# Two-layer hybrid trunk on one core: folding the two modulation vectors into one tile by partition halves before the transposes

## The chip, the cores and the metric

The kernel runs on one core of one Trainium2 chip. The metric is the device time of one execution in microseconds (us); lower is better. The kernel before takes 2441.62 us, the median of 3 runs.

## The reference

One inference step of a trunk of two layers. A layer modulates its normalised input, projects it into three parallel mixers (differential attention, mLSTM, neighbourhood attention), gates and sums their outputs, adds the result to the residual stream, and then runs a squared-ReLU MLP in the same way. There are 640 token rows: 512 of a denoising sample and 128 of a prompt, each group with its own modulation vector (conditioning `c` and `c_ctx`). Cut to what bears on the change:

```python
def layer(x, mod, lp, lam_init, ctx):
    sh1, sc1, g1, sh2, sc2, g2 = jnp.split(mod, 6, axis=-1)
    h = rmsnorm(x, lp['norm1']) * (1 + sc1) + sh1
    ...                                  # three mixers, gates -> merged
    x = x + g1 * (merged @ lp['w_out'])
    h2 = rmsnorm(x, lp['norm2']) * (1 + sc2) + sh2
    u = jnp.square(jax.nn.relu(h2 @ lp['w_ff1'] + lp['b_ff1']))
    x = x + g2 * (u @ lp['w_ff2'] + lp['b_ff2'])
```

`mod` is the product of a conditioning vector of 1024 with `w_mod` (1024 x 6144 for each layer) plus `b_mod`, once for each of the two vectors. The MLP is 1024 to 4096 to 1024.

## The kernel before

One program for one core, written with a framework that takes the order of a Python walk as a wish and lets a scheduler place the instructions on the engines. Every matrix product is split: weights and activations are kept as a rounded high part and a low rest, and each product is three matmuls (lines 191 to 193 in `gemm_a`, with the weights stationary, and 210 to 212 in `gemm_b`, with the activations stationary). A block of weights arrives as a 1 MB tile `raw`, of which there are two buffers for all loads of weights; ACT casts it to `whi` (L217) and DVE subtracts to get `wlo` (L218). Loads are issued by SP, in the order that the scheduler set.

**The modulation** is a matrix product with two columns, and it is done mostly on DVE, in the background. `mod_first` does the first 2048 columns of layer 0 at the start. The 20 chunks of 512 columns that are left (8 of layer 0, 12 of layer 1) go through `mod_chunk_dve`. For each chunk two `raw` tiles of `w_mod` are loaded (L325); each holds four slices of 128 rows by 512 columns. Into two accumulators `macc`, one for each vector, DVE adds slice times the vector's value in that row: 2 multiplications (L331) and 14 multiply-adds (L333) a chunk. What is left is the sum over the 128 partitions. PE transposes each accumulator in four blocks of 128x128 (L340, eight transposes a chunk) into a PSUM tile of the tag `t`, DVE reduces each tile along its free axis (L341, two a chunk), and `mod_store` adds the bias and writes into `modc` (L314).

The chunks are one generator, `bg`, made in `run`. Each `background()` runs it to its next `yield`. It is called from two kinds of place: in the mixers before the units whose number is in `BG_UNITS`, and in the feed-forward stage from `ff1` at the places in `FF1_BG` and from `ff2` after the row tiles in `FF2_BG`. The chunks of layer 0 run in layer 0's mixers, those of layer 1 in layer 0's feed-forward; layer 1's own stages have no background work. A chunk of layer 0 has two steps and a chunk of layer 1 four, as the `yield`s in it stand.

**The feed-forward** of a layer goes chapter by chapter. A chapter `ch` has two items `ff1(ch, 0)` and `ff1(ch, 2)`, of 4 gemms each, and a pair of items `ff2(ch, 0)` and `ff2(ch, 1)` of 5 gemms each (one for each of the five row tiles t). A gemm of ff2 is 12 matmuls of 512 columns; its result is scaled by DVE into a `tmp` tile of two buffers (L1577) and added to the residual rows by POOL (L1578). A gemm of ff1 is 24 matmuls of 256 or 384 columns; ACT applies ReLU and a square (L1490, L1491) and DVE makes the low part (L1492, L1493).

**PSUM** matters here. In this stage the gemms take their result tile alternately from the tag `t` (two buffers) and from the tag `mm` (two buffers), see `mm_ps`. The transposes of a chunk take theirs from `t` too (`t_ps`). Buffers of a tag go round in the order in which tiles are asked for, so a matmul that opens a tile waits until the engine that reads the tile two places earlier in that tag has read it. In the mixers the tag `mm` serves the projections; its tiles are read, among others, by the gates' tanh on ACT (L470, in `unit_gate`).

Of the kernel before, what the change touches and what calls it, by code (L numbers as in the profile page):

```python
# [14 lines left out]
ALU = mybir.AluOpType  # L15
AX = mybir.AxisListType
# [3 lines left out]
P = 128  # L20
# [66 lines left out]
class Builder:  # L87
# [229 lines left out]

    def mod_chunk_dve(self, l, n):

        nc, I = self.nc, self.I  # L320
        acc = [self.T(self.wp, [P, 512], F32, "macc", 2) for _ in range(2)]
        for kh in range(2):
            raw = self.T(self.wp, [P, 2048], F32, "raw", NRAW)
            r3 = raw.rearrange("p (k c) -> p k c", k=4)
            nc.sync.dma_start(r3, I["w_mod"][l, n, kh])  # L325
            for k in range(4):
                kk = kh * 4 + k
                for v in range(2):
                    s = self.cc3[:, v, kk:kk + 1]
                    if kk == 0:  # L330
                        nc.vector.tensor_scalar_mul(acc[v], r3[:, k, :], s)  # L331
                    else:
                        nc.vector.scalar_tensor_tensor(acc[v], r3[:, k, :], s, acc[v], op0=ALU.mult, op1=ALU.add)  # L333
                if kk in ((1, 3, 5) if l else (3,)):
                    yield
        red = self.st(8)
        for v in range(2):
            tp = self.t_ps()
            for j in range(4):
                nc.tensor.transpose(tp[:, j * P:(j + 1) * P], acc[v][:, j * P:(j + 1) * P], self.ident)  # L340
            nc.vector.tensor_reduce(red[:, 4 * v:4 * v + 4], tp.rearrange("p (j c) -> p j c", j=4), axis=AX.X, op=ALU.add)  # L341
        self.mod_store(l, n, red.rearrange("p (v j) -> p v j", v=2))
        yield

# [185 lines left out]
    def drive(self, units, stages, rate, w, tail, free=False):  # L530
# [41 lines left out]
        while cur[1] is not None:  # L572
# [13 lines left out]
            self.units_run += 1  # L586
            if self.units_run in BG_UNITS:
                self.background()
# [1150 lines left out]
ML_FIRST = 2  # L1739
CARRY = 3  # L1740
LAG1, LAG2 = 1, 1
FF1_BG, FF2_BG = ((0, 0), (1, 256)), (1, 3)
BG_UNITS = range(8, 42, 2)
WARM = (0, 0, 0, 0, 6, 2, 1, 1)
NSL, NOT, NV = 16, 12, 9

# [84 lines left out]
```

## Time and profile before

| | |
|---|---|
| median of 3 runs | 2441.62 us (2440.91 to 2443.32) |
| the profiled execution | 2439.98 us |
| its span in the profile | 2438.2 us |
| mean granted TensorE clock | 0.999 |
| chain that ended last, by engine | PE 91%, DVE 3%, DMA 2%, ACT 1%, issue 1%, POOL 1% |
| bytes moved by DMA | 286.51 MB, mean 118 GB/s |

All durations below come from the one profiled execution. The span is what lies between the first and the last recorded instruction; the execution's own time is 1.8 us longer, and the median of the runs is 1.6 us above that. Matmuls are pipelined: the duration of one overlaps the next, so what one costs is the distance between starts. Layer 0's feed-forward chapters lie at about 860 to 1165 us, the chapters of layer 1 that are read below at 2042 to 2320 us.

### The profile page before, as it was taken

To read this page: it belongs to the slowest core of one execution; us is meant where nothing else is said; L and a number is where in the kernel's file an instruction comes from. 1 tells how busy PE (TensorE), PEld (TensorE's weight loads), DVE (VectorE), ACT (ScalarE), POOL (GpSimd) and SP (SyncE) were. 2 spreads that over 40 slices of the span, in tenths; PEclk is the share of its full clock that TensorE was granted. 3 is DMA by queue.
4 is the path that set the end of the run, shared out by engine and by line. 5 is a ranking of instruction groups with operands and counts; after the bars stand their busy time and mean duration, and the time that the engine had idled before them with its cause. 6 is when DMAs were issued, how large, how long until landed. Compare 5 with 4: busy or idle time off the path is not lost.

```text
span 2438.2 us, 39566 instructions
## 1 busy us (share of the span) xinstructions
PE 2405.4 (99%) x15872; PEld 2260.3 (93%) x15872; DVE 1534.2 (63%) x2880; ACT 959.6 (39%) x2056; POOL 448.2 (18%) x521
## 2 busy tenths in 40 slices
PE   7999999999999999999999999999999999999998
PEld 4999999999998989999989999999999989999997
DVE  6667888667555899899475547664453564444444
ACT  4333454444434322222354325454553253222242
POOL 0011001233200333332010010102240012333301
PEclk9999999999999999999999999999999999999999
DMA  7333323433372344444233231223232722212221
GB/s 272 112 103 127 126 99 116 133 122 136 120 259 97 121 139 143 151 142 154 86 125 118 94 100 66 83 78 122 67 128 85 277 73 84 87 69 72 84 70 60
DMA packets 73703, 286.51 MB, mean 118 GB/s; under 512 B 9888, under 2 KB 21248, under 8 KB 49968
## 3 DMA queue, kind: packets, MB, share of 16 engines
q1 hardware_dynamic: 73520, 283.99, 33.6%
q8 instruction: 124, 2.03, 0.3%
q14 instruction: 59, 0.48, 0.1%
HBM read 257.60 MB, written 26.35 MB: 116 GB/s over the span
## 4 chain that ended last, share of the span: by engine, by line
PE 91%; DVE 3%; DMA 2%; ACT 1%; issue 1%; POOL 1%; SPq 0%; POOLq 0%; DVEq 0%; ACTq 0%
PE mm L191 15%; PE mm L192 14%; PE mm L193 14%; PE mm L212 5%; PE mm L211 5%; PE mm L210 5%; PE t L210 3%; PE t L212 3%; PE t L211 3%; PE t L193 3%; PE t L192 3%; PE t L191 3%; PE t L1067 2%; PE t L1356 1%; PE s L1337 1%
## 5 line engine op out<-in xcount | busy, mean ns | idle before, releaser
L191 PE MATMUL mm<-act,whi 128*128 128x384 f32 (+1 forms) x2128 | 682.4, 321 | 2.4 <-DVE act L643 2.4
L192 PE MATMUL mm<-act,whi 128*128 128x384 f32 (+1 forms) x2128 | 670.9, 315 | 0.0
L193 PE MATMUL mm<-act,wlo 128*128 128x384 f32 (+1 forms) x2128 | 670.8, 315 | 0.0
L217 ACT CAST whi<-raw 128x1024 fp32r<-128x1024 f32 x296 | 310.9, 1050 | 896.5 <-PE mm L192 420.0
L218 DVE TENSOR_TENSOR wlo<-raw,whi 128x1024 fp32r<-128x1024 f32 x296 | 377.1, 1274 | 360.5 <-ACT whi L217 306.0
L191 PEld LDWEIGHTS mm<-act,whi 128*128 128x128 f32 x2128 | 402.4, 189 | 6.7 <-DVE act L643 3.1
L192 PEld LDWEIGHTS mm<-act,whi 128*128 128x128 f32 x2128 | 402.8, 189 | 0.0
L193 PEld LDWEIGHTS mm<-act,wlo 128*128 128x128 f32 x2128 | 402.0, 189 | 0.0
L1578 POOL TENSOR_TENSOR x<-x,tmp 128x512 f32<-128x512 f32 x120 | 194.0, 1623 | 452.0 <-DVE tmp L1577 446.6
L210 PE MATMUL mm<-whi,act 128*128 128x512 f32 (+2 forms) x768 | 260.8, 340 | 0.0
L212 PE MATMUL mm<-whi,act 128*128 128x512 f32 (+2 forms) x768 | 257.3, 335 | 0.0
L211 PE MATMUL mm<-wlo,act 128*128 128x512 f32 (+2 forms) x768 | 257.2, 335 | 0.0
L333 DVE SCALAR_TENSOR_TENSOR macc<-raw,cc,macc 128x512 f32<-128x512 f32 x280 | 228.7, 859 | 21.6 <-DMA raw<-w_mod 21.4
L210 PE MATMUL t<-whi,act 128*128 128x512 f32 (+2 forms) x448 | 167.1, 373 | 0.1
L212 PE MATMUL t<-whi,act 128*128 128x512 f32 (+2 forms) x448 | 166.7, 372 | 0.0
L211 PE MATMUL t<-wlo,act 128*128 128x512 f32 (+2 forms) x448 | 166.4, 371 | 0.0
L193 PE MATMUL t<-act,wlo 128*128 128x256 f32 (+1 forms) x560 | 160.0, 286 | 0.0
L192 PE MATMUL t<-act,whi 128*128 128x256 f32 (+1 forms) x560 | 159.9, 286 | 0.0
L191 PE MATMUL t<-act,whi 128*128 128x256 f32 (+1 forms) x560 | 159.8, 285 | 0.0
L212 PEld LDWEIGHTS mm<-whi,act 128*128 128x128 f32 x768 | 145.5, 189 | 14.2
L210 PEld LDWEIGHTS mm<-whi,act 128*128 128x128 f32 x768 | 145.5, 189 | 14.1
L211 PEld LDWEIGHTS mm<-wlo,act 128*128 128x128 f32 x768 | 145.5, 189 | 14.0
(301 smaller groups left out, 4107.5 us busy)
## 6 DMA issues: line engine op xcount, KB each, us to landing
raw<-w_in SPq DMA_DIRECT2D x64, 1024.0 KB
raw<-w_ff SPq DMA_DIRECT2D x64, 1024.0 KB
raw<-w_mod SPq DMA_DIRECT2D x48, 1024.0 KB
mgd<-act SPq DMA_DIRECT2D x32, 320.0 KB
act<-mgd SPq DMA_DIRECT2D x32, 320.0 KB
raw<-w_out SPq DMA_DIRECT2D x8, 1024.0 KB
gr<-gd SPq DMA_DIRECT2D x12, 512.0 KB
act<-rd SPq DMA_DIRECT2D x16, 320.0 KB
```

What stands on the lines that cost most here:

```text
L191: nc.tensor.matmul(o, wh, ah, start=(k == 0), stop=False)
L192: nc.tensor.matmul(o, wh, al, start=False, stop=False)
L193: nc.tensor.matmul(o, wl, ah, start=False, stop=(k == nk - 1))
L210: nc.tensor.matmul(o, ah, wh, start=(first and k == 0), stop=False)
L211: nc.tensor.matmul(o, ah, wlo, start=False, stop=False)
L212: nc.tensor.matmul(o, al, wh, start=False, stop=(last and k == nk - 1))
L217: self.nc.scalar.copy(hi, src)
L218: self.nc.vector.tensor_tensor(lo, src, hi.bitcast(F32), op=ALU.subtract)
L333: nc.vector.scalar_tensor_tensor(acc[v], r3[:, k, :], s, acc[v], op0=ALU.mult, op1=ALU.add)
L1067: nc.tensor.matmul(ops[:, :P], pT[:, j * P:(j + 1) * P], v[:, hsl], start=(j == 0), stop=(j == nb - 1))
L1337: nc.tensor.transpose(tps[:w, j, bi * P:(bi + 1) * P], zs[j][:, o:o + w], self.ident)
L1578: nc.gpsimd.tensor_tensor(xs[t][:, sl], xs[t][:, sl], tmp, op=ALU.add)
```

## The change

After the multiply-adds of a chunk the two accumulators are folded into one tile. ACT copies partitions 64 to 127 of accumulator 0 onto partitions 0 to 63 of a scratch area, and partitions 0 to 63 of accumulator 1 onto its partitions 64 to 127; the scratch area is the first slice of the chunk's second `raw` tile. DVE adds the halves: afterwards `acc[0]` holds, on its first 64 partitions, partial sums of vector 0, and on the last 64 partial sums of vector 1. That is the end of a step. In the next step of the background four transposes, not eight, bring the tile into one PSUM tile of the tag `t`, and one reduce, not two, sums each block's two halves.

For that extra step `FF2_BG` gets three places a pair item in place of two, and `BG_UNITS` 25 units in place of 17 (a chunk of layer 0 has three steps now, one of layer 1 five). In the changed file lines 320 to 336 stand one lower than before, and what follows `mod_chunk_dve` stands 7 lower; so L1577 before is L1584 after.

```diff
                 if kk in ((1, 3, 5) if l else (3,)):
                     yield
+        s, up, dn = r3[:, 0, :], slice(0, 64), slice(64, P)
+        nc.scalar.copy(s[up], acc[0][dn])
+        nc.scalar.copy(s[dn], acc[1][up])
+        nc.vector.tensor_tensor(acc[0][up], acc[0][up], s[up], op=ALU.add)
+        nc.vector.tensor_tensor(acc[0][dn], acc[1][dn], s[dn], op=ALU.add)
+        yield
         red = self.st(8)
-        for v in range(2):
-            tp = self.t_ps()
-            for j in range(4):
-                nc.tensor.transpose(tp[:, j * P:(j + 1) * P], acc[v][:, j * P:(j + 1) * P], self.ident)
-            nc.vector.tensor_reduce(red[:, 4 * v:4 * v + 4], tp.rearrange("p (j c) -> p j c", j=4), axis=AX.X, op=ALU.add)
+        tp = self.t_ps()
+        for j in range(4):
+            nc.tensor.transpose(tp[:, j * P:(j + 1) * P], acc[0][:, j * P:(j + 1) * P], self.ident)
+        nc.vector.tensor_reduce(red.rearrange("p (v j) -> p v j", v=2), tp.rearrange("p (j v c) -> p v j c", j=4, v=2),
+                                axis=AX.X, op=ALU.add)
...
-FF1_BG, FF2_BG = ((0, 0), (1, 256)), (1, 3)
-BG_UNITS = range(8, 42, 2)
+FF1_BG, FF2_BG = ((0, 0), (1, 256)), (0, 2, 4)
+BG_UNITS = (8, 10, 12, 14, 16, 18, 20, 22, *range(24, 41))
```

**PE, layer 0's feed-forward, where an ff2 pair ends and the next chapter's ff1 begins.** `t` and `mm` are the PSUM tiles, `macc` an accumulator, `act` activations, `whi` and `wlo` weights. Before, PE goes from the last gemm of ff2 straight into the first gemm of ff1, and four transposes of accumulator 0 come behind that gemm, four of accumulator 1 one matmul later:

```order
L193 MATMUL t_9811<-act_8248,wlo_9722 128x256
L340 MATMUL t_9846<-ident_78,macc_9679 128x128 x4
L191 MATMUL mm_9869<-act_8234,whi_9721 128x384
L340 MATMUL t_9852<-ident_78,macc_9680 128x128 x4
L192 MATMUL mm_9869<-act_8235,whi_9721 128x384
```

Now, at such a boundary (all six between chapters 0 and 6 look like it):

```order
L211 MATMUL mm_10292<-wlo_10125,act_9805 128x512
L212 MATMUL mm_10292<-whi_10124,act_9806 128x512
L346 MATMUL t_10309<-ident_78,macc_10160 128x128 x4
L191 MATMUL t_10324<-act_8218,whi_10228 128x256
L192 MATMUL t_10324<-act_8219,whi_10228 128x256
```

The four transposes stand between the last gemm of ff2 and the first of ff1, so their tile `t_10309` is asked for before the tile `t_10324` of ff1's first gemm. The other chunk of each chapter has its four transposes behind the first gemm of `ff2(ch, 0)`, where before it had eight behind the second.

**DVE, the ff2 pair ahead of that same boundary, from the scaling of its fifth result to the scaling of its ninth.** `tmp<-t` or `tmp<-mm` is the scaling of one ff2 result, L334 and L332 the multiply-adds and the multiplication of a chunk, L340 and L341 the two adds of the fold:

```order
L1584 TENSOR_TENSOR tmp_10197<-t_10184,gr_8214 128x512
L218 TENSOR_TENSOR wlo_10229<-raw_10226,whi_10228 128x1024
L218 TENSOR_TENSOR wlo_10233<-raw_10226,whi_10232 128x1024
L1584 TENSOR_TENSOR tmp_10217<-mm_10204,gr_8212 128x512
L340 TENSOR_TENSOR macc_10160<-macc_10160,raw_10220 64x512
L341 TENSOR_TENSOR macc_10160<-macc_10161,raw_10220 64x512
L1584 TENSOR_TENSOR tmp_10249<-t_10236,gr_8212 128x512
L332 TENSOR_SCALAR macc_10354<-raw_10356,cc_89 128x512
L1584 TENSOR_TENSOR tmp_10265<-mm_10252,gr_8212 128x512
L334 SCALAR_TENSOR_TENSOR macc_10354<-raw_10356,cc_89,macc_10354 128x512 x3
L1584 TENSOR_TENSOR tmp_10289<-t_10276,gr_8212 128x512
```

The seventh result (`t_10236`) and the ninth (`t_10276`) are the two tiles of the tag `t` ahead of `t_10309` and `t_10324`; the next chunk's first multiplication and three multiply-adds stand between their scalings. The load of `raw_10356` waits for the second L218 of `raw_10226`.

**ACT, layer 0's mixers, one of the eight chunks there.** L477 is the tanh that empties a projection's tile `mm` (L470 before), L338 and L339 are the copies of the fold:

```order
L217 CAST whi_7074<-raw_7072 128x1024
L477 ACTIVATE act_6799<-mm_6800,hbias_159 128x256
L1354 COPY act_6645<-s_1150_6832 128x384
L338 COPY raw_7025<-macc_6787 64x512
L339 COPY raw_7025<-macc_6788 64x512
L217 CAST whi_7078<-raw_7072 128x1024
L477 ACTIVATE act_6799<-mm_6845,hbias_159 128x384
```

The two copies are new; they stand ahead of a cast and of the next evacuation of an `mm` tile.

## Rows read from the trace of the kernel before

**Rows 1.** The page, part 1: busy time, share of the span and instructions of each engine.

```profile
PE 2405.4 (99%) x15872; PEld 2260.3 (93%) x15872; DVE 1534.2 (63%) x2880; ACT 959.6 (39%) x2056; POOL 448.2 (18%) x521
```

**Rows 2.** The waits of PE: line, what it waited for; us in total, times, longest us.

```profile
PE mm L191 <- ACT act L470: 1.8, 2, 1.1
...
PE t L340 <- DVE tmp L1577: 0.8, 1, 0.8
...
PE t L340 <- DVE act L1069: 0.4, 1, 0.4
```

**Rows 3.** Timeline of PE: first gemm of four feed-forward chapters (start us, us, instruction).

```profile
958.95 0.28 PE L191 MATMUL t<-act,whi 128*128 128x256 f32 x1
...
1131.47 0.28 PE L191 MATMUL t<-act,whi 128*128 128x256 f32 x1
...
2042.83 0.28 PE L191 MATMUL t<-act,whi 128*128 128x256 f32 x1
...
2319.73 0.28 PE L191 MATMUL t<-act,whi 128*128 128x256 f32 x1
```

**Rows 4.** Timeline of PE: one batch of transposes between two gemms of ff1.

```profile
961.70 0.28 PE L193 MATMUL t<-act,wlo 128*128 128x256 f32 x1
961.82 0.60 PE L340 MATMUL t<-ident,macc 128*128 128x128 f32 x4
962.17 0.42 PE L191 MATMUL mm<-act,whi 128*128 128x384 f32 x1
```

**Rows 5.** Lines by form: a reduce, an ACT copy, a DVE add of 64x512 (ns min/median/max).

```profile
L341 DVE TENSOR_REDUCE st<-t x40: 669/680/694, 223.7 to 1165.1; 128x4 f32<-128x512 f32 x40
...
L970 ACT CAST stk<-act x32: 602/618/621, 261.3 to 1816.1; 64x512 fp32r<-64x512 f32 x32
...
L975 DVE TENSOR_TENSOR act<-act,stk x32: 670/689/849, 262.3 to 1817.6; 64x512 fp32r<-64x512 f32 x32
```

**Rows 6.** Windows: busy us (instructions) by engine, one feed-forward period.

```profile
936.10:993.65 57.55, 57.55 (x330) 52.28 (x329) 53.33 (x73) 15.80 (x24) 20.59 (x11) 1.00 0.42 146
```

**Rows 7.** Timeline of PE: last gemm of an ff2 pair and the gemm after it.

```profile
1013.75 0.39 PE L210 MATMUL mm<-whi,act 128*128 128x512 f32 x1
...
1016.47 0.28 PE L191 MATMUL t<-act,whi 128*128 128x256 f32 x1
```

**Rows 8.** Timeline of DVE in that same ff2 pair [idle before <-releaser].

```profile
993.91 0.69 DVE L1577 TENSOR_TENSOR tmp<-mm,gr 128x512 f32<-128x512 f32 x1 [1.76 <-PE mm L212]
...
995.72 0.54 DVE L331 TENSOR_SCALAR macc<-raw,cc 128x512 f32<-128x512 f32 x1
...
996.65 2.06 DVE L333 SCALAR_TENSOR_TENSOR macc<-raw,cc,macc 128x512 f32<-128x512 f32 x3
...
1004.03 1.21 DVE L218 TENSOR_TENSOR wlo<-raw,whi 128x1024 fp32r<-128x1024 f32 x1
1005.17 0.68 DVE L1577 TENSOR_TENSOR tmp<-t,gr 128x512 f32<-128x512 f32 x1
...
1007.91 3.13 DVE L333 SCALAR_TENSOR_TENSOR macc<-raw,cc,macc 128x512 f32<-128x512 f32 x3 [0.33 <-DMA raw<-w_mod]
1010.97 0.68 DVE L1577 TENSOR_TENSOR tmp<-t,gr 128x512 f32<-128x512 f32 x1
...
1014.60 0.68 DVE L1577 TENSOR_TENSOR tmp<-mm,gr 128x512 f32<-128x512 f32 x1
...
1017.56 0.68 DVE L1577 TENSOR_TENSOR tmp<-t,gr 128x512 f32<-128x512 f32 x1
```

**Rows 9.** The chain that ended last, two of its loads (start us, us, what).

```profile
505.00 6.57 DMA raw<-w_mod
...
886.99 4.68 DMA raw<-w_mod
```

**Rows 10.** Lines by form, window 860 to 1170: the residual adds on POOL.

```profile
L1578 POOL TENSOR_TENSOR x<-x,tmp 128x512 f32<-128x512 f32 x50 | 88.6, 1778 | 187.7 <-DVE tmp L1577 187.7
```

**Rows 11.** Timeline of PE: a stop in the mixers.

```profile
267.66 0.39 PE L191 MATMUL mm<-ot,whi 128*128 128x256 f32 x1 [1.08 <-ACT act L470]
```

## The prediction

> **What bounds the kernel now.** I began with the busy times of the engines. PE is busy for 2405.4 of the span's 2438.2 us, DVE for 63%, ACT for 39% and POOL for 18% [rows 1]. Because matmuls are pipelined and each lasts longer than the distance to the next, I did not take the 99% as proof and read the waits of PE next: outside the chain of scalar steps in the mixers it stands still for very little, and the transposes' own stops come to 1.2 us in two waits [rows 2]. So PE's work sets the end nearly everywhere. Two things can move the time then: work taken off PE, and a new stop of PE. Then I read the timeline of PE and DVE in layer 0's feed-forward, where 12 of the 20 chunks run, since the new order puts four transposes into a critical place there, and the windows by engine for that stretch. DVE is busy there for 53.33 of a period of 57.55 us [rows 6], so it has 4.2 us of slack a period, and it is late: the ninth scaling of an ff2 pair ends at 1018.24 [rows 8], 1.77 us after PE has begun ff1's first gemm at 1016.47 [rows 7].
>
> **What the change takes away.** Each chunk has four transposes fewer, 80 in all. Two prices for one come from rows. A feed-forward period with 16 of them lasts (1131.47 - 958.95)/3 = 57.51 us; in layer 1, with none, (2319.73 - 2042.83)/5 = 55.38 us [rows 3]. The difference, 2.13 us, is 0.133 us a transpose, so 80 give 10.6 us. By the batch, a single batch of four sets the next matmul back from 961.82 to 962.17, by 0.35 us [rows 4]; a period then keeps two such batches, 0.70 us, in place of 2.13, which is 1.43 us for two chunks and 14.3 us for 20. The two may not be added. Some of the 1.2 us of stops ahead of transposes [rows 2] goes too, and may come back with other neighbours. I take 12 us. Each chunk's second reduce goes as well, 0.680 us of DVE [rows 5]; that is cover, not path.
>
> **What it adds.** Each chunk gets two ACT copies and two DVE adds of 64x512. Casts and adds of that shape take 0.618 and 0.689 us in the mixers [rows 5]. ACT has 1.24 us a chunk more and is busy for 15.80 of 57.55 us [rows 6]; DVE has 1.38 - 0.68 = 0.70 us more, against its 4.2 us of slack for two chunks. Taken as work, both cost nothing; what covers them is PE's gemms, and where a copy or an add stands ahead of something PE waits for, the cover is gone. There are two such places. The extra steps carry no instructions of their own: POOL's order is untouched, and on SP only the w_mod loads change place. The load of ff1's weights now stands behind two of them; by the count below its buffer comes free at about 8 us of the ff2 pair, a load takes 4.68 us [rows 9], and DVE has split it by 21.7, where PE wants it at 27.9, so I cost it at nothing.
>
> **The boundary from ff2 to ff1.** Six times the transposes now come between ff2's last gemm and ff1's first. The transposes take the `t` tile that the seventh scaling frees. The first gemm of ff1 takes the one freed by the ninth, where before it took the seventh's. So PE stops until DVE has finished the ninth scaling. How late is that? I count from the pair's start. A gemm of ff2 lasts 1016.47 - 1013.75 = 2.72 us [rows 7], and there are now two batches of 0.35 us in the way, so the first gemm of ff1 could start at 10 x 2.72 + 0.70 = 27.9. DVE's chain, by the new order:
> - The second gemm ends at 5.8. The scaling of its result stands behind a reduce, a multiplication and two multiply-adds; I start it at 6.7.
> - From one scaling to the next with three multiply-adds between is 1014.60 - 1010.97 = 3.63 us [rows 8]. Three such steps bring the fifth scaling to 17.6.
> - Two L218 follow, 0.6 + 2 x 1.21, and one clash with POOL. That clash is 3.13 - 2.06 = 1.07 us, the price of the same three multiply-adds beside L1578 and without it [rows 8]. The second L218 ends between 20.6 (no clash) and 21.7.
> - Only that end frees the buffer for the next chunk's w_mod load, 4.68 us [rows 9]: it lands between 25.3 and 26.4. The sixth scaling, the adds and the seventh fit in before.
> - The multiplication (0.54) waits for that load, then the eighth scaling and three multiply-adds take 3.63 more, and the ninth scaling 0.68 [rows 8]: done between 30.2 and 31.2, and up to 0.7 later if the multiplication meets POOL, whose residual adds are on for 1.78 us each [rows 10].
>
> PE therefore stops for 2.3 to 4.0 us; I take 3.5, towards the upper end, because seven of POOL's adds fall into this stretch and I charged one clash to the L218s. Six boundaries give **21 us**. The lower bound is the lag of before: with the ninth scaling ending 1.77 us after the boundary and one batch of 0.35 us ahead, 1.42 us, or 8.5 us for six. The upper bound takes the longest load of the chain, 6.57 in place of 4.68 us [rows 9]: 3.5 + 1.9 = 5.4 us, or 32 us.
>
> Here the Trainium skill's page "SBUF — State Buffer" ("Who interferes with whom") bears on the clash: a DVE instruction with two inputs in SBUF contends with a GpSimd instruction that reads SBUF, and whoever is late is blocked fully, while a reduce on trn2 does not contend. The multiply-adds' 2.06 against 3.13 us agree. By that rule the fold's adds can be held up too, where the reduce they replace was not; the seventh scaling would come later but still ahead of the load, so the sum stays at 21, and what it could change is the second rival below.
>
> **The mixers.** Eight folds run in layer 0's mixers. The trace has one stop there of PE behind ACT's tanh, 1.08 us [rows 11], so evacuations of `mm` can be late by a little. Two copies ahead of one are at most 1.24 us, so the bounds are 0 and 8 x 1.24 = 9.9 us. I take 1.5, nearest to that one stop of before plus a little, since ACT is idle for most of the time and most copies find a gap.
>
> **The sum** for the profiled execution: 2439.98 - 12 + 21 + 1.5 = 2450.5 us. The median of the runs lies 1.6 us above it, so the forecast is **2452 us**, about 0.4% slower.
>
> **The rivals.**
> - *Faster: the boundary's wait is covered.* If DVE's ninth scaling is done by 27.9, only the 12 us count: 2441.6 - 12 + 1.5 = 2431 us. For it: the fold spreads a chunk over more steps, and DVE loses a reduce. Against: DVE was 1.77 us late at that place in the kernel before, and the load between the sixth and eighth scalings is not earlier. It would need the ninth scaling 3 us earlier than I count. Chance 0.06.
> - *Faster, by less: DVE becomes the bound.* Without a stop of PE at the boundary, DVE's period would be 53.33 + 2 x 0.70 + 2 x 1.07 (both folds' adds beside POOL) = 56.9 us, against 57.55 - 1.24 = 56.3 us for PE. DVE then takes 0.6 us of each of six periods: 2431 + 4 = 2435 us. It rests on the clash of the adds with POOL, which no row of before shows for this shape; the nearest, the multiply-adds, show it [rows 8]. Chance 0.04. The skill's rule named above is what would make it so, the adds having two SBUF inputs and the reduce none that contends.
> - *No change: a smaller stop.* Between 1.2 and 2.8 us a boundary (7 to 17 us) the stop gives back the 12 us: 2437 to 2446 us. For it: my start for the second scaling is rough, and each clash fewer is 1.07 us. Chance 0.16.
> - *Much slower: the mixers pay as well.* With the upper bound at the boundary or most copies in front of an evacuation, 2439.98 + 1.6 - 11 + 24 to 32 + 5 to 10 is 2460 to 2473 us. Chance 0.14.
> - *The change doesn't do what it says*: the extra steps could overrun, and the rest of the chunks be drained at the end of the feed-forward. 25 units are 8 x 3 + 1 steps, and the last instructions of the modulation stand in the order where they stood, so I give it nothing.
>
> **How the numbers follow.** The forecast, a stop of 2.8 to 4.5 us a boundary, 2446 to 2460 us, has 0.60. Differences within 0.2%, 4.9 us, are about what a measurement of this kernel can't tell from none. Faster is 0.06 + 0.04 = 0.10; slower is 0.60 + 0.14 = 0.74, the rest same. The forecast's own range is 2446 to 2460. The full bounds are 2439.98 + 1.6 - 15.5 + 8.5 = 2435 and 2439.98 + 1.6 - 10.6 + 32 + 9.9 = 2473; leaving out one in ten on each side gives 2438 to 2465.
>
> **What would show it.** In the profile after, the waits of PE should list ff1's first gemm (`t`, L191) waiting for DVE's scaling L1584, six times, 3 to 4 us each, and none of it in layer 1. The period of the feed-forward should be 57.5 - 1.4 + 3.5 = 59.6 us. The transposes should be 80, in 20 batches. DVE should idle just ahead of L332 in the boundary's pair, for the w_mod load. The prediction is wrong if the six stops are missing, or if PE waits as long elsewhere, for an ACT evacuation in the mixers first of all.

## The result, and the profile after

The changed kernel takes 2487.83 us (median of 4 runs, 2486.78 to 2490.14) against 2441.93 us: a ratio of 1.0187, 95% interval 1.0175 to 1.0199, 45.9 us slower. Forecast were 2452 us and a range up to 2465 us. The sign was right, the size was not: 46 us in place of 10, and 12.6 of them in the mixers, where the forecast had next to nothing.

The profiled execution has a span of 2486.0 us, 47.8 us longer. Set by the same marks in both timelines, the first gemm of layer 0's ff1 starts 12.6 us later (798.2 against 785.6), and the stretch from there to layer 1's first gemm on a tile `t` is 33.3 us longer (529.4 against 496.1). The last 1.9 us lie in layer 1, which the change doesn't touch. So **the mixers lost 12.6 us and layer 0's feed-forward 33.3 us**; the forecast had 1.5 us for added waits in the mixers, and 21 us for the boundaries.

The page's first part answers to [rows 1]:

```profile
PE 2413.2 (97%) x15792; PEld 2268.3 (91%) x15792; DVE 1555.2 (63%) x2900; ACT 984.7 (40%) x2096; POOL 439.0 (18%) x521
```

DVE is busy for 21 us more, ACT for 25, and PE for 8 although it has 80 transposes less to do. The waits of PE (us in total, times, longest) answer to [rows 2]:

```profile
PE t L191 <- DVE tmp L1584: 18.8, 4, 5.5
...
PE t L191 <- ACT whi L217: 9.7, 2, 5.1
PE s L1320 <- POOL act L969: 6.0, 2, 5.7
...
PE mm L191 <- DVE act L1237: 3.3, 2, 2.4
...
PE mm L191 <- DVE act L526: 2.0, 1, 2.0
PE mm L191 <- ACT act L477: 1.9, 2, 1.2
```

The first two rows are one thing: ff1's first gemm waits at the six boundaries (the two that are put down to a cast of ACT start 0.15 us after the ninth scaling too, like the others). On the timeline of PE they are these, all with the first gemm of ff1 behind the transposes:

```profile
860.54 0.55 PE L191 MATMUL t<-act,whi 128*128 128x256 f32 x1 [4.36 <-DVE tmp L1584]
...
924.95 0.55 PE L191 MATMUL t<-act,whi 128*128 128x256 f32 x1 [5.14 <-DVE tmp L1584]
...
988.35 0.55 PE L191 MATMUL t<-act,whi 128*128 128x256 f32 x1 [5.46 <-DVE tmp L1584]
...
1051.58 0.55 PE L191 MATMUL t<-act,whi 128*128 128x256 f32 x1 [4.63 <-ACT whi L217]
...
1113.19 0.55 PE L191 MATMUL t<-act,whi 128*128 128x256 f32 x1 [3.82 <-DVE tmp L1584]
...
1177.51 0.55 PE L191 MATMUL t<-act,whi 128*128 128x256 f32 x1 [5.09 <-ACT whi L217]
```

They sum to 28.5 us. The duration behind the start shows a second thing: the 128x256 matmul takes 0.55 us where it took 0.28 [rows 3]. The windows by 2 us around the third stop (us, then the busy time of PE, PEld, DVE, ACT, POOL, then the granted clock, the share of the DMA engines, GB/s) show why:

```profile
984.00:986.00 2.00, 0.00 (x0) 0.00 (x0) 1.96 (x2) 1.59 (x2) 1.92 (x2) 1.00 0.00 0
986.00:988.00 2.00, 0.00 (x0) 0.00 (x0) 2.00 (x2) 0.40 (x1) 1.05 (x1) 0.54 0.00 0
988.00:990.00 2.00, 1.65 (x8) 1.68 (x9) 2.00 (x4) 0.00 (x0) 1.72 (x1) 0.50 0.00 0
...
992.00:994.00 2.00, 2.00 (x13) 2.00 (x13) 1.86 (x3) 0.46 (x1) 0.00 (x0) 0.75 0.00 0
994.00:996.00 2.00, 2.00 (x14) 2.00 (x13) 1.50 (x4) 0.43 (x2) 0.00 (x0) 1.00 0.92 262
```

PE stands still from 982.9 on, the granted clock falls in that time to 0.50, which is the lower of its two levels (1.2 of 2.4 GHz), and it comes back some 5 us after PE has started again. By the distance between matmuls (0.21 us in place of 0.12 for 256 columns), PE ran at the lower level for some 26 us behind the six stops together, which cost it some 12 us. 28.5 + 12 less some 7 us for the 48 transposes that the feed-forward lost is the 33 us by which that stage is longer. That is how the time is made up on PE; what it would take to get it back is another question, which the experiments answer.

DVE's timeline ahead of the stop at 988.35, the same stretch as the second half of [rows 8]:

```profile
977.12 0.67 DVE L340 TENSOR_TENSOR macc<-macc,raw 64x512 f32<-64x512 f32 x1
977.83 1.68 DVE L341 TENSOR_TENSOR macc<-macc,raw 64x512 f32<-64x512 f32 x1
979.54 0.69 DVE L1584 TENSOR_TENSOR tmp<-t,gr 128x512 f32<-128x512 f32 x1
981.43 0.49 DVE L332 TENSOR_SCALAR macc<-raw,cc 128x512 f32<-128x512 f32 x1 [1.20 <-DMA raw<-w_mod]
981.83 0.69 DVE L1584 TENSOR_TENSOR tmp<-mm,gr 128x512 f32<-128x512 f32 x1
982.43 5.17 DVE L334 SCALAR_TENSOR_TENSOR macc<-raw,cc,macc 128x512 f32<-128x512 f32 x3
987.52 0.68 DVE L1584 TENSOR_TENSOR tmp<-t,gr 128x512 f32<-128x512 f32 x1
```

The pair's first gemm began at 954.56. Counted from there the seventh scaling starts at 25.0, the multiplication waits for its w_mod load until 26.9, the eighth scaling starts at 27.3, and the ninth ends at 33.6. The forecast's chain had the ninth done between 30.2 and 31.9; its steps and their order are there. The three multiply-adds ahead of the ninth scaling took 5.17 us, not 3.13, because two of POOL's additions fell beside them, the second one of 128x1024 (L1575).

The period between the second and the third of those stops, 63.4 us, answers to [rows 6]; the forecast had 59.6, and the five whole periods have 63.4 on average:

```profile
924.95:988.35 63.40, 57.94 (x321) 52.89 (x321) 56.55 (x76) 18.43 (x28) 19.44 (x12) 0.96 0.39 133
```

DVE is busy for 56.55 us of it, against 53.33 in a period of before. By form in that window:

```profile
L334 DVE SCALAR_TENSOR_TENSOR macc<-raw,cc,macc 128x512 f32<-128x512 f32 x28 | 26.2, 959 | 0.1
...
L332 DVE TENSOR_SCALAR macc<-raw,cc 128x512 f32<-128x512 f32 x4 | 3.7, 914 | 1.2 <-DMA raw<-w_mod 1.2
...
L341 DVE TENSOR_TENSOR macc<-macc,raw 64x512 f32<-64x512 f32 x2 | 2.4, 1182 | 0.1
...
L340 DVE TENSOR_TENSOR macc<-macc,raw 64x512 f32<-64x512 f32 x2 | 1.3, 674 | 0.0
```

The two additions of the fold are 3.7 us a period, one of them 1.18 us on average because it is held up by POOL; the first multiplications of a chunk (L332) went from 0.49 to 0.91 us, since they moved next to POOL's additions; the two reduces that went away give back 1.4.

In the mixers PE's stops (those of 0.1 us or more, from 180 us on) sum to 14.1 us against 3.0 before, and the granted clock was 0.50 behind three of them, which cost at most 5 us of work. With the 4.3 us of 32 transposes taken off that makes up nearly all of the 12.6 us there.

### The profile page after: what moved, and what is told of

Its sections match the earlier page's. It is cut to its first block, busy times and chain, and to the rows that moved or that the text cites. A ratio compares the mean times of both kernels' runs of the same rounds, so it can differ in the third digit from the quotient of the medians.

```text
span 2486.0 us, 39483 instructions
## 1 busy us (share of the span) xinstructions
PE 2413.2 (97%) x15792; PEld 2268.3 (91%) x15792; DVE 1555.2 (63%) x2900; ACT 984.7 (40%) x2096; POOL 439.0 (18%) x521
## 4 chain that ended last, share of the span: by engine, by line
PE 62%; DVE 7%; DMA 3%; issue 2%; ACT 1%; POOL 1%; SPq 0%; POOLq 0%; DVEq 0%; ACTq 0%
PE mm L191 10%; PE mm L192 10%; PE mm L193 10%; PE mm L210 3%; PE mm L211 3%; PE mm L212 3%; PE t L191 3%; PE t L192 3%; PE t L193 3%; PE t L212 3%; PE t L210 3%; PE t L211 3%; DMA raw<-w_mod 2%; DVE macc L334 2%; DVE wlo L218 1%
## 5 line engine op out<-in xcount | busy, mean ns | idle before, releaser
L218 DVE TENSOR_TENSOR wlo<-raw,whi 128x1024 fp32r<-128x1024 f32 x296 | 376.0, 1272 | 370.5 <-ACT whi L217 316.5
L334 DVE SCALAR_TENSOR_TENSOR macc<-raw,cc,macc 128x512 f32<-128x512 f32 x280 | 232.4, 853 | 7.5 <-DMA raw<-w_mod 6.2
L191 PE MATMUL t<-act,whi 128*128 128x256 f32 (+1 forms) x560 | 165.9, 296 | 28.5 <-DVE tmp L1584 18.8
L192 PE MATMUL t<-act,whi 128*128 128x256 f32 (+1 forms) x560 | 165.0, 295 | 0.0
L210 PEld LDWEIGHTS mm<-whi,act 128*128 128x128 f32 x768 | 145.6, 190 | 14.1
```

Source lines behind the costliest of these rows:

```text
L191: nc.tensor.matmul(o, wh, ah, start=(k == 0), stop=False)
L192: nc.tensor.matmul(o, wh, al, start=False, stop=False)
L210: nc.tensor.matmul(o, ah, wh, start=(first and k == 0), stop=False)
L218: self.nc.vector.tensor_tensor(lo, src, hi.bitcast(F32), op=ALU.subtract)
```

## Experiments

Each run is told by its time and by two stretches of its trace: "mixers" is the start of layer 0's first ff1 gemm, "FF" the distance from there to layer 1's first gemm on a tile `t`. Ratios are against the kernel before on the same chip, with the 95% interval.

| kernel | time, us | ratio | mixers | FF |
|---|---|---|---|---|
| before | 2441.9 | 1 | 785.6 | 496.1 |
| after | 2487.8 | 1.0187 [1.0175, 1.0199] | 798.2 | 529.4 |
| s2 in FF | 2473.8 | 1.0126 [1.0111, 1.0141] | 796.8 | 514.1 |
| old mixers | 2475.3 | 1.0131 [1.0116, 1.0146] | 787.0 | 527.0 |
| s2 in FF, old mixers | 2460.0 | 1.0073 [1.0056, 1.0090] | 786.0 | 514.2 |
| fill | 2489.7 | 1.0194 [1.0179, 1.0209] | 796.5 | 530.9 |
| FF: fold alone | 2464.2 | 1.0088 [1.0073, 1.0104] | 786.4 | 520.1 |
| FF: steps alone | 2444.8 | 1.0009 [1.0000, 1.0018] | 787.6 | 499.1 |
| mixers: fold alone | 2460.7 | 1.0074 [1.0057, 1.0091] | 784.8 | 515.1 |
| mixers: steps alone | 2461.6 | 1.0079 [1.0064, 1.0094] | 787.5 | 515.3 |
| sums by ones | 2458.8 | 1.0072 [1.0059, 1.0085] | 793.8 | 504.2 |
| scratch in PSUM | 2453.9 | 1.0049 [1.0036, 1.0063] | 787.4 | 508.0 |
| scratch in PSUM, relief | 2441.5 | 0.9999 [0.9990, 1.0008] | 786.1 | 495.2 |
| before, relief | 2441.5 | 1.0001 [0.9992, 1.0010] | 786.2 | 496.2 |
| before, added load | 2444.1 | 1.0009 [1.0000, 1.0018] | 785.5 | 498.3 |
| after, relief | 2479.9 | 1.0156 [1.0141, 1.0171] | 798.5 | 521.8 |
| s2 in FF, relief | 2467.5 | 1.0103 [1.0088, 1.0119] | 797.3 | 512.4 |
| s2 in FF, mixers' scratch in PSUM | 2458.0 | 1.0063 [1.0049, 1.0076] | 781.1 | 514.6 |
| scratch in PSUM, more relief | 2440.7 | 0.9992 [0.9983, 1.0001] | 785.5 | 495.3 |
| all three | 2439.9 | 0.9988 [0.9978, 0.9998] | 782.7 | 497.4 |

**1. The boundary's tile from another tag.** My theory was the prediction's: the tag `t` going round makes the stops. The rival was that DVE is late in any case.

```diff
-        tp = self.t_ps()
+        tp = self.s_ps()[:, :512] if l else self.t_ps()
```

> The transposes of the feed-forward's 12 chunks open a tile of the PSUM tag s2, which nothing else uses in that stage, in place of one of the tag t; the order of every engine stays that of the changed kernel. Theory A (the six stops come from the tag t going round, and the half clock behind them from the stops): the six waits of ff1's first gemm vanish and so do the stretches at half clock, 28.5 + 12 us, so 2487.8 - 40.5 = 2447 us, and the feed-forward period becomes about 56.5 us. Theory B (DVE is simply late, and the next gemms of ff1 wait in its place): stops of 1 to 3 us a boundary come back at the second or third gemm of ff1, 2455 to 2475 us.

The six stops are gone (one of 0.40 us is left), and 14 us of the 40 came back. PE now waits in the middle of each chapter, not at ff1's next gemms as theory B had it, for the activations of ff1 that the first gemm of ff2 multiplies:

```profile
946.30 0.49 PE L210 MATMUL t<-whi,act 128*128 128x512 f32 x1 [1.80 <-ACT act L1498]
...
948.46 0.79 PE L212 MATMUL t<-whi,act 128*128 128x512 f32 x1 [1.42 <-DVE act L1500]
```

L1498 and L1500 are the last steps on ff1's results on ACT and DVE. So theory B holds for the larger part: the tag is the cause of where PE stops, not of how much.

**2. The mixers as before**, `if l == 0` with the old transposes and `BG_UNITS = range(8, 42, 2)`.

> Layer 0's eight chunks as in the kernel before (two steps, eight transposes, 17 units), the feed-forward as changed. Theory A (the mixers' part of the change costs 12.6 us by itself, the distance by which the first boundary is late): 2487.8 - 12.6 = 2475 us, all of it ahead of the first feed-forward chapter. Theory B (that delay is of the run and not of the change): 2488 us.

As theory A had it: 12.5 us, and the stretch before ff1 is back at 787. The two stages cost separately.

**3. Both.**

> Both together: the fold is kept in the feed-forward alone, with its transposes in the tag s2. If the two costs are separate and are all there is, what is left is the saving of 48 transposes, 6.4 to 8.6 us: 2434 to 2436 us, and a period of 56.1 to 56.5 us. If DVE becomes the bound in the feed-forward without the stops, the period stays at 57 us or above and the time at 2439 or above.

2460, 18 us slower than before, with a fold in 12 chunks and no stop over 0.44 us at the boundary. A period of it:

```profile
934.92:997.79 62.87, 58.69 (x321) 52.41 (x321) 56.68 (x76) 18.04 (x29) 19.54 (x11) 0.97 0.39 134
```

62.9 us, and DVE is busy for 56.68 of them. Its waits in that period, and then those in the period of [rows 6] of the kernel before:

```profile
DVE wlo L218 <- ACT whi L217: 3.0, 2, 2.3
DVE macc L334 <- DMA raw<-w_mod: 1.6, 1, 1.6
DVE macc L332 <- DMA raw<-w_mod: 1.3, 1, 1.3
```

```profile
DVE macc L333 <- DMA raw<-w_mod: 2.0, 1, 2.0
DVE tmp L1577 <- PE mm L212: 1.8, 1, 1.8
DVE wlo L218 <- ACT whi L217: 0.2, 1, 0.2
```

Before, 1.8 of the 4.2 us were a wait for PE. Now none is: DVE waits for w_mod loads and for ACT's casts, in its own order. On PE the 18 us are mostly stops, 16 us more of them than before, 14 of these for ff1's activations as in run 1. Behind them some 6 us of work are lost at the lower clock, about what the 48 transposes had taken.

**4. The stops filled with work.** 32 unused transposes behind the four at each boundary.

> The changed kernel with 32 more transposes (their result isn't used) behind the four at each of the six boundaries, which fill some 4 us of each stop with work of PE; the wait for the ninth scaling stays. Theory A (the clock falls because PE stands still): the stops shrink to under 1 us each, the first gemm of ff1 starts as late as before, and the matmuls behind it go at full clock, so 12 us come back: 2476 us. Theory B (the half clock behind the boundary has another reason): 2488 us or, with the added work, more.

The stops were cut down, but not all under 1 us:

```profile
858.83 0.35 PE L191 MATMUL t<-act,whi 128*128 128x256 f32 x1 [0.89 <-DVE tmp L1589]
...
922.35 0.55 PE L191 MATMUL t<-act,whi 128*128 128x256 f32 x1 [3.29 <-DVE tmp L1589]
...
1048.61 0.36 PE L191 MATMUL t<-act,whi 128*128 128x256 f32 x1 [0.64 <-ACT whi L217]
```

At three of the six boundaries no matmul behind was slow any more (the duration at 858.83 is 0.35, not 0.55). Nothing came back in time: at three boundaries PE still stopped for 1.9 to 3.3 us, and in two chapters it stopped for 2.85 and 1.19 us ahead of an ff2 gemm, where the changed kernel does not. Theory A fell: some 6 of the 12 us of work were no longer lost at the lower clock, and the time did not fall. What the clock costs by itself the run doesn't tell, since the added work has its own time.

**5 and 6. Fold or steps, in the feed-forward.** Fold alone: no `yield` of its own, `FF2_BG = (1, 3)`. Steps alone: `yield` ahead of eight old transposes, `FF2_BG = (0, 2, 4)`. Both with the transposes in `s2` and the old mixers, so that run 3 is the two together.

> Layer 0's chunks as before. In the feed-forward the fold is kept (four transposes, in s2) but in the step where the transposes stand, with four steps a chunk and FF2_BG (1, 3) as before. Theory A (the fold's own work on DVE, 1.9 us more a chunk by the two traces, is what makes DVE the bound): 2452 to 2460 us, near the 2460 of fold and steps together. Theory B (the extra step is what costs: the places of the steps, and with them the order of the loads): 2434 to 2443 us, the fold then saves its transposes.

> The other half: layer 0's chunks as before; in the feed-forward no fold (eight transposes and two reduces, in s2), but the transposes in a step of their own, five steps a chunk and FF2_BG (0, 2, 4). Theory A (the fold's work): 2441 to 2445 us. Theory B (the places of the steps): 2452 to 2465 us.

The fold alone costs 21.5 us, 4 more than theory A's upper end, the steps alone 2.1. Without its own step the transposes stand where DVE has not finished the additions, and PE waits for them directly:

```profile
909.74 1.09 PE L355 MATMUL s<-ident,macc 128*128 128x128 f32 x4 [4.53 <-DVE macc L351]
...
972.22 0.63 PE L355 MATMUL s<-ident,macc 128*128 128x128 f32 x4 [3.35 <-DVE macc L351]
```

(L351 is the second addition there.) The own step moved this stop to the boundary; it didn't make it.

**7 and 8. Fold or steps, in the mixers**, each with the feed-forward of run 1. Neither alone is the mixers' cost.

> The mixers' half of the same question; the feed-forward is as changed, with its transposes in s2, in which layer 0's old chunks gave 2460 and its changed ones 2474 us. Here layer 0's chunks have the fold, but two steps and the 17 units of before. Theory A (the extra step and the closer units make the w_mod loads late, and DVE stands in front of them): 2455 to 2460 us. Theory B (the fold itself, with its copies on ACT and the raw buffer that it holds): 2470 to 2475 us.

> As the run before it, the other way round: layer 0's chunks have three steps and the 25 units, but no fold. Theory A (steps and units): 2472 to 2480 us. Theory B (the fold): 2458 to 2462 us.

Both give what the old mixers gave (2460.0), together they cost 14 us (2473.8). Both theories fall; the cause needs the two at once. The trace of the changed kernel shows it: DVE's rows (idle time ahead, and what ended it) and, a little later, PE's three longest stops in the mixers.

```profile
535.85 0.48 DVE L332 TENSOR_SCALAR macc<-raw,cc 128x512 f32<-128x512 f32 x1 [7.59 <-DMA raw<-w_mod]
...
576.05 1.16 DVE L527 TENSOR_TENSOR act<-act,act 128x256 f32<-128x256 f32 x2 [4.52 <-DMA act<-mgd]
...
635.11 0.48 DVE L332 TENSOR_SCALAR macc<-raw,cc 128x512 f32<-128x512 f32 x1 [4.63 <-DMA raw<-w_mod]
```

```profile
538.71 0.41 PE L191 MATMUL mm<-act,whi 128*128 128x384 f32 x1 [2.38 <-DVE act L1237]
...
579.78 0.79 PE L1320 MATMUL s<-act,act 128*128 128x128 f32 x2 [5.68 <-POOL act L969]
...
637.31 0.39 PE L191 MATMUL mm<-ot,whi 128*128 128x256 f32 x1 [2.03 <-DVE act L526]
```

DVE stands in front of the first multiplication of a chunk until the w_mod load lands, 7.59 and 4.63 us, and what PE needs (the evacuations L1237 and L526) stands behind it. The middle row is a load of another kind (`mgd`) that was late; `vb` below is a further input of the mixers. In SP's order it stood behind a load of `vb`, in front of which SP had waited 13.0 us for POOL; PE's middle stop, behind POOL, follows from these two. Why are loads late? The fold's scratch is the raw tile's first slice, so the buffer is held until the second addition (L341), and with units one apart the next load wants it sooner. Among the waits of SP between 480 and 660 us stands this one, for a load of weights (L141) that has a load of `vb` and then the w_mod load of the third row behind it:

```profile
SPq L141 <- DVE macc L341: 9.6, 1, 9.6
```

For the first row the rows show less: its w_mod load found its buffer free, but went out only at 527.64, behind a load of `vb` and right behind the load of the weights `w_up_da`. So the held buffer was, up to here, a theory.

**9. That theory, tested:** the scratch of the mixers' fold is a PSUM tile.

```diff
-        s, up, dn = r3[:, 0, :], slice(0, 64), slice(64, P)
+        s, up, dn = r3[:, 0, :] if l else self.t_ps(), slice(0, 64), slice(64, P)
```

> As the run with s2 in the feed-forward (2474 us), and in the mixers the scratch of the two copies is a PSUM tile of the tag t, so that the raw buffer is free when its last multiply-add is done. Neither the fold nor the steps alone cost the mixers' 14 us. If both are needed because the fold holds the raw buffer and the closer units want it sooner, the 14 us come back: 2458 to 2463 us. If it is anything else (ACT's copies, DVE's adds in front of what PE waits for), 2470 us or more, the more so as the scratch takes turns with other tiles of t.

15.7 us came back. The mixers end at 781.1, 4.5 us before the kernel before, about what 32 transposes cost at 0.133 us. DVE's waits at the first multiplication, mixers only, in the changed kernel and in this one:

```profile
DVE macc L332 <- DMA raw<-w_mod: 20.7, 5, 7.6
```

```profile
DVE macc L332 <- DMA raw<-w_mod: 10.0, 3, 3.6
```

SP's wait for L341 is gone, and the load of `w_up_da` goes out at 512.90, 14 us sooner and ahead of the loads of `vb`; the load of `mgd` stands ahead of a `vb` load as well. The edit also gives the additions one SBUF input less, but that is not what helped here: in the changed kernel's mixers none of the eight second additions took more than 0.70 us. So the held buffer costs the time, partly by the wait and partly by the places that other loads get in SP's order; the run doesn't divide these two.

**10. The scratch in PSUM in the feed-forward** (tag `s2`, old mixers; run 3 otherwise).

> The fold in the feed-forward alone with its transposes in s2 (2460 us), but the scratch of the two copies is a PSUM tile of s2 in place of the raw tile's first slice. The adds then have one input in SBUF only, and the raw buffer is free when the last multiply-add has read it. If the clash of the adds with POOL and the held buffer are what costs, 2445 to 2452 us; if it is the places of the steps, 2457 to 2461 us.

6.1 us better than run 3, between the two ranges, and 12 us are left: the clash of the additions with POOL and the held buffer are a part of it, which the run doesn't divide. By the rows the 12 second additions took 14.2 us in run 3 and 8.3 here, so the clash alone could be most of the 6.1.

**11 to 13. DVE relieved, and loaded.** One of ff1's two squarings goes from DVE to ACT, in layer 0; it is some 4 us of DVE a period.

```diff
-        nc.vector.tensor_tensor(r, r, r, op=ALU.mult)
+        if l == 0:
+            nc.scalar.activation(r, r, AF.Square)
+        else:
+            nc.vector.tensor_tensor(r, r, r, op=ALU.mult)
```

> The fold in the feed-forward alone with its scratch in PSUM and its transposes in s2 (2454 us), and in layer 0's ff1 the second square (relu times relu, 0.4 to 0.55 us, eight a period) goes from DVE to ACT: about 4 us a period less for DVE. Theory A (DVE's time sets the period; the fold pays nothing because it adds to DVE): the stops go, the period falls to 56.1 to 56.5 us and what is left is the saving of 48 transposes: 2433 to 2437 us, faster than the kernel before. Theory B (late loads or the places of the steps set it): 2450 to 2455 us.

> The control: the kernel before with the same square on ACT. PE has next to no stops there, so theories A and B both expect no change, 2440 to 2443 us; were it faster, the relief would pay by itself.

> The kernel before with one useless DVE addition of 128x512 (two SBUF inputs, 0.7 to 1.2 us) behind each of layer 1's 12 chunks, PE's work unchanged. If the 4.2 us of idle time of DVE in a period are room that work can use, two additions fit in and nothing changes: 2441 to 2444 us. If DVE is at its limit in the feed-forward already, each adds its time: 12 x 0.7 to 1.2, 2450 to 2456 us.

Run 10 falls by 12.3 us with it, the kernel before by nothing: with the fold DVE's work is the limit, without it PE's. The square also stands in front of the activations for which PE waits in run 3, so whether DVE's total counts or its lateness at that place, these runs don't separate. It did not reach the 2433 to 2437 us of theory A: four stops of 0.7 to 1.9 us for DVE were left.

In run 13 the 12 added additions took 10.4 us by their rows, 1.7 a period, and cost 2.4 in all, at the edge of the noise. The trace has the cost at two places, where transposes waited for a tile of the tag `t` (842.9 to 1133.6 us; before it was 0.8 once [rows 2]):

```profile
PE t L342 <- DVE tmp L1579: 3.0, 2, 1.6
```

In the other periods the 1.7 us fitted in whole. So much of DVE's idle time could take work; more than 1.7 us a period was not tried.

**14. The changed kernel with the same relief.**

> The changed kernel as it is (transposes in t at the boundary, raw tile as scratch), with the square on ACT. If the stop at the boundary is there because DVE is short of time over the period, it shrinks to under 1.5 us and the feed-forward's 33 us come back for the most part: 2455 to 2462 us, the mixers' 14 us being left. If it comes from the order at that place, the load behind the second L218 and the three multiply-adds ahead of the ninth scaling, it stays at 3 us or more and the time at 2475 us or above.

8 us, and the boundary's stops stay:

```profile
922.81 0.55 PE L191 MATMUL t<-act,whi 128*128 128x256 f32 x1 [4.24 <-DVE tmp L1587]
...
986.71 0.50 PE L191 MATMUL t<-act,whi 128*128 128x256 f32 x1 [4.69 <-DVE tmp L1587]
```

The six are 3.7 us on average, against 4.75. Two of them are 2.7 us, the other four 3.8 to 4.7. So that wait comes for the larger part from the order at the place, as the forecast had it, and not from DVE's total.

**15. Both limits eased**, `s2` and relief, and **16, all three**, with the scratch in PSUM in both stages as well (`self.s_ps()[:, :512] if l else self.t_ps()`).

> The changed kernel with its transposes in s2 in the feed-forward (2474 us) and the square on ACT (2480 us with the transposes in t): both limits of the feed-forward eased at once. If the order at the boundary and DVE's time are two limits of nearly one height, of which the other shows when one is taken away, both together give back what neither does alone: the feed-forward is left with 0 to 5 us of its 33, and the time is that of the mixers' 14 us, 2455 to 2461 us. If a third thing holds it, 2468 us or more.

> The changed kernel with its steps, units and fold in both stages, and the three causes taken away together: the transposes in s2 in the feed-forward, the scratch in PSUM in both stages (s2 in the feed-forward, t in the mixers), the square on ACT. If the three are all of the 46 us, 2440 to 2445 us, as the fold in the feed-forward alone with the same three (2441.5). If the mixers have a further cause, 2450 us or more.

Two were not enough: 2467.5 with FF 512.4. With the scratch in PSUM the whole 46 us are gone. The kernel with the change's fold, steps and units is then 0.12% faster than before, at the edge of what the runs can tell.

**17. Other ways.** The sum over partitions by matmuls with two columns of ones, no transposes and no reduces, on the kernel before:

> A way that does without transposes, reduces and fold: the kernel before, with its steps, but the sum over the partitions by eight matmuls a chunk that have a 128x128 block of an accumulator as weights and two columns of ones as the moving side; DVE adds the bias straight from PSUM. If DVE's time is what the feed-forward is short of, this gives DVE 1.36 us a chunk back (two reduces of 0.68), and PE does no more than before: 2430 to 2441 us. If a matmul of two columns costs more than a transpose of 128, up to 0.23 us (the 128x2 matmuls at the start, which run at a lower clock), it is slower than before by up to 16 us, 2458 us.

Slower by 17 us: a period is 59.0 us, not 57.5, with nothing of PE waiting. The source has 160 two-column matmuls, and the trace shows 320: each of them stands there twice, and each of the 320 is 0.11 us behind the one before, as a transpose is. First all of them, then one batch of eight and the next gemm:

```profile
L342 PE MATMUL t<-ones,macc x320: 165/251/272, 222.6 to 1180.7; 128*128 128x2 f32 x160
```

```profile
913.08 1.88 PE L342 MATMUL t<-ones,macc 128*128 128x2 f32 x16
914.82 0.42 PE L191 MATMUL mm<-act,whi 128*128 128x384 f32 x1
```

From the batch to the next gemm it takes 1.74 us; eight transposes in one batch take 0.79 in the kernel before.

And run 11 with one of the two first multiplications on ACT too:

> The fold in the feed-forward with scratch in PSUM and the square on ACT equals the kernel before (2441.5 us), with four stops of 0.7 to 1.9 us left that wait for DVE. Here one of a chunk's two first multiplications (0.5 to 0.9 us) goes to ACT too. If DVE's time is still the limit, the stops go and it becomes faster than both kernels: 2434 to 2439 us. If ACT, which then waits for the w_mod load in its own order, makes ff1's tiles late, 2442 to 2450 us.

No difference from the kernel before; its interval ends at 1.0001. The FF stretch is 495.3 us, as in run 11, so this relief gave nothing more. The mixers of run 9 with the feed-forward of before, which by the two stretches should be some 4 us faster than before, was not tried.

## Why the prediction was wrong

**Term by term.** The sum for the profiled execution was 2450.5 us; it took 2487.8, which is 37.3 more. In the mixers the sum has 1.5 us less 32 of the 80 transposes, -3.3 us, and the trace +12.6: 15.9 of the 37.3. At the boundary it has 21 us and the trace 28.5: 7.5. For the lower clock behind those stops it has nothing and the trace 12. The last 1.9 us lie in layer 1.

**The steps that failed** are three. The first is the mixers' term: it priced the copies in front of an evacuation, and took the raw tile as scratch and the loads' new places for nothing. The second is the stops, which were taken to cost their own length. The third is "DVE has 0.70 us more, against its 4.2 us of slack for two chunks. Taken as work, both cost nothing." It does not show as a term of its own in the changed kernel, where the boundary's stops cover it, but it would have cost 18 us without them: so much longer is FF with the boundary's stop taken away (run 3), and the fold alone is enough for it (run 5). The work is not 0.70 us a chunk: DVE's busy time rose by 3.2 us a period, 1.6 a chunk, for the second addition and the multiplications that moved next to POOL's additions got longer. And the 4.2 us were not all slack: only 1.8 of them were a wait for PE.

**The rival that named this** (DVE becomes the bound) had a chance of 0.04 and a price of 0.6 us a period, on the faster side. Its mechanism held, as far as runs 11 and 12 show it; its size did not. It has 62.9 us in run 3 where the sum had 56.9: 56.68 busy, near enough, and 6.2 us of waits that I took for time to fill. Adding all the idle time of before to the new busy time gives 4.2 + 56.9 = 61.1, near the 61.6 that run 3's five whole periods have on average. But that is no rule: it would charge run 13 with all its 10.4 us, and it cost 2.4.

**The boundary** was right in place, number and cause: six stops, none in layer 1, the ninth scaling behind three multiply-adds behind a late load. 4.75 us a stop lies within the bounds of 1.4 to 5.4, but the 3.5 was too low: at the third stop by a second clash, 5.17 us for three multiply-adds where 3.13 was taken, and at the fourth, where they took 3.20, because the second scaling started 8.2 us after the pair's start and not 6.7. What I did not see is that the boundary and DVE's time are two limits of like height (33 us with both, 18 without the first, 26 with the second eased), so that 21 us was the price of one and would not have been saved by removing it.

**The clock** was not in the sum. The kernel before has a mean granted clock of 0.999 and no such stop in layer 0, and I took stops of 3 to 5 us to cost their own length. The trace has some 12 us more. Run 4 did not get them back, so what removing them alone would be worth is open.

**The mixers** had 1.5 us, with bounds 0 to 9.9, for ACT's copies in front of an evacuation. They ended 12.6 us later, by another way: DVE in front of evacuations, waiting for loads that are late because of the held buffer (run 9). The forecast had not asked, at "the scratch area is the first slice of the raw tile", who waits for that tile. It also read SP's and POOL's orders wrongly: "POOL's order is untouched, and on SP only the w_mod loads change place" does not hold in the mixers, where the trace has loads of `w_in`, `w_up_ml`, `vb` and `mgd` in other places than before, and some of POOL's work with them.

**The saving** was right in size where it could be seen: 4.5 us for 32 transposes in run 9's mixers, 0.14 us each (0.9 us of it are shorter stops of PE), and 56.3 us in the shortest period of run 16 against 57.5.

**What the range missed.** The bounds took 32 us for the boundary and 9.9 for the mixers, 2473 us in all; no bound had the clock or the buffer. Two inner bounds are also 2 us off by the sum's own terms: 2.8 us a boundary gives 2448 us and not 2446, and 4.5 gives 2458 and not 2460.

## What to carry to other kernels

An engine that is busy for 92% of a period is not 8% free for certain: look at what its idle time waits for. The part that is a wait for the engine that sets the pace is room; whether the rest is, a run with useless work added tells, with about as much of it as the change adds. Here 1.7 us a period cost next to nothing, and the fold's 3.2 cost 18 us in all. When a scratch area is cut from a buffer that is loaded round and round, the price is that buffer's next load, the loads that are issued behind it, and whatever stands behind the instructions that wait for them. When a stop is removed, ask what the next limit would be before counting the stop as gain: here removing the boundary's stop gave 14 us of 40.

## What the runs showed of the hardware

- TensorE's granted clock fell to 0.50 within stops of 3.8 to 5.5 us and stayed there for 2.9 to 6.2 us behind each; in the stretch shown it was back between 992 and 994, some 5 us after the restart. In the mixers it fell behind stops of 2.4 and 2.0 us as well.
- A DVE addition of 64x512 with two SBUF inputs took 0.67 us alone and 1.68 at most beside POOL; a multiplication of 128x512 with one SBUF input took 0.49 us and, in the rows of the feed-forward, 0.91 on average and 1.55 at most where it had moved next to POOL's additions. The Trainium skill's page "SBUF — State Buffer" ("Who interferes with whom") names both cases, two SBUF inputs and a `tensor_scalar` in a two-port mode; of these my sum for the work charged none, and the one for the boundary one clash and part of another.
- A two-column matmul with a 128x128 fp32 accumulator as weights cost PE more than a transpose of the same block, 1.5 us a period for 16 of them: it stands in the trace as two instructions, 0.11 us apart like transposes.
